# RWKV groups in rounds of three lanes, in one written order on four engines, with an inverse that adds nothing on VectorE

## Chip, cores and metric
The kernel runs on one core of a Trainium2 chip, as one program. The metric is the time of one execution on the device in microseconds (us). The engines are TensorE (PE: matmuls, transposes through the identity; PEld is its weight load), VectorE (DVE), ScalarE (ACT), GpSimd (POOL) and SyncE (SP, which issues the loads of weights).

## What is computed
Two blocks of a network run one after the other over 256 tokens. `first_block` is a feed-forward part, a mixing part and another feed-forward part; the mixing part is attention beside a bidirectional RWKV-7, whose outputs are put side by side and multiplied by `w_out`. The change lies in RWKV-7. Its recurrence over the tokens, for every head and both directions, is

```python
def _rwkv7_step(state, inp):
    r, w, k, v, kk, kka = inp
    sa = einsum('dbhvk,dbhk->dbhv', state, kk)
    state = state * w[..., None, :] - sa[..., :, None] * kka[..., None, :] + v[..., :, None] * k[..., None, :]
    y = einsum('dbhvk,dbhk->dbhv', state, r)
    return state, y
```

with 8 heads of 64, `w` a decay per token and channel (from `wd`, `w2`), `a` a sigmoid (from `ad`, `a2`), `kk` the normalized `k * k_k` and `kka = kk * a`. The two directions are summed, normalized per head (`lnx`), a bonus `v * sum(r * r_k * k)` is added, and all is gated by `sigmoid(gd) @ g2`. `second_block` uses modulation vectors, products of the conditioning `c` with `w_mod`, of which those of its first layer are computed beside the RWKV part.

## The kernel before
**The stage.** `mix1` runs RWKV (`rwkv`) woven with side work: `weave(self.rwkv(...), side, 4)` takes one step of `side` after every four of RWKV's, and what is left of `side` follows. The side work is `mod(0)`: 12 column blocks, each with two loads of 1 MB of `w_mod` (L133, on SP's queue, into `wraw`, which has three buffers), eight matmuls of 32 columns of weights by 512 (L837, four to a load, into the `md` tag of PSUM), a copy `mrow` on ACT (L840), four transposes (L843) and small sums on DVE. Then comes the product with `w_out`: eight loads of 512 KB, each cast by ACT (`whi`, L149) and split by DVE (`wlo`, L150), and 12 matmuls of 512 columns for each (L160 to L162), into `md` and `c2`. Behind it stand a norm and the next feed-forward part.

**The groups.** RWKV is cut into four tiles of 128 channels (`ct`, two heads each) and two directions (`d`), eight groups. A group works on 256 tokens in four chunks of 64. It makes the decay and `a` (matmuls L569 and L570, tanh L573, sigmoid L574, scan L577, exponentials L581 to L591; d=0 also transposes `v` and makes `kk` through two copies `kex`, L558, with a matmul each, L559), products of these (AR, BK, nB, Kh, L594 to L608), and LM, the masked products within a chunk (eight matmuls L623, masks L626). Then it inverts a triangular 64 by 64 matrix for each head and chunk: POOL masks the first level (L654), DVE adds the identity (L656) and transposes (L657), and five levels follow. Each level is two batches of eight quarter matmuls (64 by 64): L663, whose result DVE masks to `FT` (L665), and L670, whose result DVE adds to X (L672) and transposes (L673); the last one adds to Y (L675). Products with the inverse (L680 to L716) follow, and when both directions of a tile are done `finish` runs the chunks' states (L733 to L748), the norm (L751 to L760, with a power on POOL), `fo` (L768 to L770) and the split `xhi`, `xlo` that `w_out` multiplies.

**What sets the order.** The groups are written one after the other with `chain`. The program's scheduler orders the instructions of each engine by its own costs, within the limits of the buffers: the PSUM tags c0, c1, c2, two buffers each, go to the groups in turn by `(2 * ct + d) % DEEP`, with `DEEP = 3`. So work of up to three groups, the side work and `finish` is mixed by the scheduler on each engine's queue, and each engine runs its queue in the order that came out.

Of the kernel before, what the change touches and what calls it, by code (L numbers as in the profile page):

```python
# [20 lines left out]
S = 256  # L21
# [5 lines left out]
LAG = 3  # L27
# [6 lines left out]
class Builder:  # L34
# [473 lines left out]
    def rwkv(self, mp, me, R, yT):  # L508
# [30 lines left out]
        def group(ct, d, sh):  # L539
            tag = "c%d" % ((2 * ct + d) % DEEP)  # L540
            r, k, v = rkv[:, ct], rkv[:, 4 + ct], rkv[:, 8 + ct]
            cc = slice(ct * 128, ct * 128 + 128)
            if d == 0:
                VN = mp.tile([128, 2, 128], F32, name="VN", bufs=2)

                RQ = mp.tile([128, 2, 2, 4, 64], F32, name="RQ", bufs=2)
                vp = self.psum(2, 128, tag=tag)
                for t in range(2):
                    nc.tensor.transpose(vp[:, t], v[:, t * 128:t * 128 + 128], self.ident)
                nc.scalar.copy(VN, vp)  # L550
                for c in range(2):
                    nc.scalar.copy(RQ[halves[1 - c], :, c].rearrange("p d u b -> p d (u b)"),
                                   vp[halves[c]].rearrange("p a b -> p (a b)")[:, None, :].to_broadcast([64, 2, 256]))
                kk = tmpt("kk", 2)
                np_ = self.psum(2, 128, tag=tag)
                for t in range(2):
                    ex = me.tile([128, 2, 64], F32, name="kex", bufs=1)
                    nc.scalar.copy(ex, rn[:, ct, t][:, :, None].to_broadcast([128, 2, 64]))  # L558
                    nc.tensor.matmul(np_[:, t], ex.rearrange("p a b -> p (a b)"), self.ident, start=True, stop=True)  # L559
                nc.vector.scalar_tensor_tensor(kk, k, self.v("rwkv_k_k", ct), np_.rearrange("p a b -> p (a b)"),  # L560
                                               op0=OP.mult, op1=OP.mult)
                sh.update(kk=kk, kds=[], VN=VN, RQ=RQ, Rp=mp.tile([128, 2, 2, 128], F32, name="Rp", bufs=2),
                          y=mp.tile([128, 2, 2, 64], F32, name="y", bufs=2), bv=mp.tile([128, S], F32, name="bv", bufs=2),
                          PZ=mp.tile([128, 2, 3, 2, 64], F32, name="PZ", bufs=2),
                          WC=mp.tile([128, 2, 4], F32, name="WC", bufs=2))
            kk, kds, VN, RQ, PZ, y = (sh[n] for n in ("kk", "kds", "VN", "RQ", "PZ", "y"))
# [8 lines left out]
            sig, a = sa[:, 0], sa[:, 1]  # L575
            cs = tmpt("cs")
            nc.vector.tensor_tensor_scan(cs, rst, sig, 0.0, op0=OP.mult, op1=OP.add)  # L577
            E = me.tile([128, 3, S], F32, name="E")
# [4 lines left out]
            nc.vector.tensor_tensor(less, cs, sig, op=OP.subtract)  # L583
            nc.vector.tensor_tensor(c4(rest), tot.to_broadcast([128, 4, 64]), c4(cs), op=OP.subtract)
            if d == 0:
                nc.scalar.copy(Winc, cs)
            else:
                nc.vector.tensor_tensor(Winc, Wexc, sig, op=OP.add)
            Winv = tmpt("Winv", 2)
            nc.scalar.activation(Winv, Winc, AF.Exp, scale=-KAPPA)  # L590
            nc.scalar.activation(E, E, AF.Exp, scale=KAPPA)  # L591
            kd = tmpt("kd", 2)
            nc.scalar.activation(kd, a, AF.Identity, scale=self.v("rwkv_k_a", ct), bias=ka1[:, ct:ct + 1])
            nc.vector.tensor_tensor(kd, kd, k, op=OP.mult)  # L594
            kds.append(kd)
            nc.gpsimd.tensor_tensor(a, a, kk, op=OP.mult)
            AR = mp.tile([128, 2, 2, 128], F32, name="AR", bufs=3)
            nc.vector.tensor_tensor(AR[:, :, 0], t2v(kk), t2v(Wexc), op=OP.mult)
            nc.vector.tensor_tensor(AR[:, :, 1], t2v(r), t2v(Winc), op=OP.mult)

            BK2 = me.tile([128, 2, 256], F32, name="BK2", bufs=2)
            ch = lambda t: t.rearrange("p (a c b) -> p a c b", c=2, b=64)
            nc.vector.tensor_tensor(BK2.rearrange("p t (j b) -> p t j b", b=64)[:, :, 0:4:3], ch(a), ch(Winv), op=OP.mult)
            nc.vector.tensor_tensor(BK2[:, :, 64:192], t2v(kd), t2v(Winv), op=OP.mult)
            nB = tmpt("nB", 2)
            nc.vector.tensor_tensor(nB, a, Wrem, op=OP.mult)
            Kh = tmpt("Kh", 2)
            nc.gpsimd.tensor_tensor(Kh, kd, Wrem, op=OP.mult)  # L608
            yield

            RHS = mp.tile([128, 4, 128], F32, name="RHS", bufs=DEEP)
            tp = self.psum(2, 2, 64, tag=tag)
            for t in range(2):
                nc.tensor.transpose(tp[:, t].rearrange("p a b -> p (a b)"), AR[:, t, 0], self.ident)
            nc.scalar.copy(RHS.rearrange("p (t h) c -> p t h c", t=2)[:, :, :, 0:64], tp)

# [8 lines left out]
            for hh in range(2):  # L625
                nc.vector.tensor_tensor(LM[:, hh:4:2].rearrange("p t m b -> p t (m b)"), lps[hh],  # L626
                                        lmm[:, d].rearrange("p c m b -> p (c m b)")[:, None, :].to_broadcast([128, 2, 256]), op=OP.mult)
            yield
            tp = self.psum(4, 128, tag=tag)
# [6 lines left out]
            if d == 1:  # L636
                s = tmpt("ksum")
                nc.gpsimd.tensor_tensor(s, kds[0], kds[1], op=OP.add)
                nc.vector.scalar_tensor_tensor(s, s, rk5[:, ct:ct + 1], r, op0=OP.mult, op1=OP.mult)
                bp = self.psum(S, tag=tag)  # L640
                nc.tensor.matmul(bp, blk, s, start=True, stop=True)
                nc.vector.tensor_tensor(sh["bv"], bp, v, op=OP.mult)
            lv = self.psum(4, 64, tag=tag)
            for u in range(4):
                for c in range(2):
                    o = halves[1 - c]
                    nc.tensor.matmul(lv[halves[c], u], LM[o, u, 2 * c], RQ[o, d, c, u], start=True, stop=True)
            nc.scalar.copy(RHS[:, :, 64:128], lv)
# [4 lines left out]
            for c in range(2):  # L653
                nc.gpsimd.tensor_tensor(Y[halves[c]], LM[halves[c], :, 2 * c],  # L654
                                        lvl[halves[c], 0][:, None, :].to_broadcast([64, 4, 64]), op=OP.mult)
            nc.vector.tensor_tensor(Y, Y, over(6), op=OP.add)  # L656
            nc.vector.transpose(X, Y)  # L657
            for li in range(1, 6):
                fp = self.psum(4, 64, tag=tag)
                for u in range(4):  # L660
                    for c in range(2):
                        ps = halves[c]
                        nc.tensor.matmul(fp[ps, u], LM[ps, u, 2 * c], X[ps, u], start=True, stop=True)  # L663
                F = square("FT")
                nc.vector.tensor_tensor(F, fp, over(li), op=OP.mult)  # L665
                yp = self.psum(4, 64, tag=tag)
                l, r_ = (Y, F) if li < 5 else (F, Y)
                for u in range(4):
                    for ps in halves:
                        nc.tensor.matmul(yp[ps, u], l[ps, u], r_[ps, u], start=True, stop=True)  # L670
# [837 lines left out]
def chain(*gens):  # L1508
    for g in gens:
        yield from g  # L1510
# [183 lines left out]
```

## Time and profile before

| | |
|---|---|
| median of three runs | 2453.7 us (2453.59 to 2454.38) |
| profiled execution, its own time | 2451.68 us |
| its span | 2449.9 us |
| PE busy over the span | 2346.6 us (96%) |
| DVE, ACT, POOL busy | 1614.4, 1307.0, 188.2 us |
| mean granted TensorE clock | 0.986 |

The span is from the first to the last instruction. Busy time is a share of all stages together; for a change of one stage the windows of that stage count (the first rows below). Matmuls are pipelined and their ends are modelled, so where a matmul's cost is wanted, the step from one start to the next is safer than its length. Idle time in brackets stands before an instruction and names what ended it.

### The profile page before, as it was taken

What the parts mean: (1) busy time and instruction counts of PE and PEld (TensorE: products, weight loads), DVE (VectorE), ACT (ScalarE), POOL (GpSimd) and SP (SyncE); (2) the same over time, 40 slices, a digit from 0 to 9 for tenths busy, and PEclk for the clock granted to TensorE, in tenths of its full rate; (3) what the DMA queues carried; (4) which work ended last, traced back from release to release, by engine and by line L of the source; (5) the groups of instructions that cost most, each with busy time, mean ns of one, the idle gap of its engine ahead of it and who ended that gap; (6) DMA issues with size and microseconds to landing.
All of it is one profiled execution on the core that took longest, in us unless ns stands there. A gap on an engine that the chain in (4) does not pass through costs nothing. (4 is left out here: it accounts for less than half of the span.)

```text
span 2449.9 us, 38791 instructions
## 1 busy us (share of the span) xinstructions
PE 2346.6 (96%) x15592; PEld 1963.8 (80%) x15592; DVE 1614.4 (66%) x2427; ACT 1307.0 (53%) x2038; POOL 188.2 (8%) x248
## 2 busy tenths in 40 slices
PE   7998989979998999999999999989999999999996
PEld 7996866659998767799899886778888887788875
DVE  5555667656547466443333464669989989889897
ACT  5543644345545355433223243567887777777764
POOL 0001112110001000200100110020100110020000
PEclk9999999999999999999999999999999999999998
DMA  8654342275652350232322235469999999999993
GB/s 261 198 187 138 122 162 88 81 237 170 202 173 88 102 172 21 70 118 82 110 93 82 83 113 175 135 237 373 335 352 341 343 345 335 352 339 335 365 343 134
DMA packets 281100, 489.56 MB, mean 200 GB/s; under 512 B 11424, under 2 KB 116896, under 8 KB 280912
## 3 DMA queue, kind: packets, MB, share of 16 engines
q1 hardware_dynamic: 280832, 486.80, 58.2%
q8 instruction: 124, 2.03, 0.3%
q14 instruction: 64, 0.52, 0.1%
q0 software_dynamic: 80, 0.21, 0.0%
HBM read 485.92 MB, written 1.05 MB: 199 GB/s over the span
## 5 line engine op out<-in xcount | busy, mean ns | idle before, releaser
L150 DVE TENSOR_TENSOR wlo<-wraw,whi 128x1024 fp32r<-128x1024 f32 (+1 forms) x830 | 975.5, 1208 | 227.9 <-ACT whi L149 221.9
L149 ACT CAST whi<-wraw 128x1024 fp32r<-128x1024 f32 (+1 forms) x832 | 824.6, 1030 | 257.9 <-PE ps L162 102.2
L161 PE MATMUL gu<-xlo,whi 128*128 128x256 f32 x1408 | 394.4, 280 | 4.0 <-DVE xlo L193 2.4
L160 PE MATMUL gu<-xhi,whi 128*128 128x256 f32 x1408 | 394.6, 281 | 0.8 <-ACT xhi L200 0.8
L162 PE MATMUL gu<-xhi,wlo 128*128 128x256 f32 x1408 | 393.8, 280 | 0.0
L161 PE MATMUL gu<-wlo,X 128*128 128x512 f32 (+1 forms) x768 | 291.2, 379 | 4.4 <-DVE wlo L150 3.4
L162 PE MATMUL gu<-whi,X 128*128 128x512 f32 (+1 forms) x768 | 286.2, 373 | 0.0
L160 PE MATMUL gu<-whi,X 128*128 128x512 f32 (+1 forms) x768 | 285.1, 374 | 0.0
L161 PEld LDWEIGHTS gu<-xlo,whi 128*128 128x128 f32 x1408 | 264.8, 188 | 5.3 <-DVE xlo L193 2.9
L160 PEld LDWEIGHTS gu<-xhi,whi 128*128 128x128 f32 x1408 | 264.7, 188 | 2.2 <-ACT xhi L200 1.4
L162 PEld LDWEIGHTS gu<-xhi,wlo 128*128 128x128 f32 x1408 | 265.2, 188 | 0.0
L161 PEld LDWEIGHTS gu<-wlo,X 128*128 128x128 f32 x768 | 144.7, 188 | 45.5 <-DVE wlo L150 21.3
L160 PEld LDWEIGHTS gu<-whi,X 128*128 128x128 f32 x768 | 144.7, 188 | 25.5
L162 PEld LDWEIGHTS gu<-whi,X 128*128 128x128 f32 x768 | 144.7, 188 | 23.6
L274 DVE TENSOR_TENSOR hh<-sg,gu 128x256 f32<-128x256 f32 x88 | 36.8, 418 | 164.6 <-ACT sg L272 164.6
L161 PE MATMUL acc<-wlo,xhi 128*128 128x512 f32 (+1 forms) x368 | 141.8, 386 | 3.1 <-DVE wlo L150 3.1
L160 PE MATMUL acc<-whi,xhi 128*128 128x512 f32 (+1 forms) x368 | 140.8, 385 | 2.5 <-ACT whi L149 1.1
L162 PE MATMUL acc<-whi,xlo 128*128 128x512 f32 (+1 forms) x368 | 141.6, 385 | 0.1
L161 PE MATMUL dn<-wlo,hT 128*128 128x512 f32 x352 | 140.6, 399 | 0.0
L162 PE MATMUL dn<-whi,hT 128*128 128x512 f32 x352 | 138.6, 394 | 0.0
L160 PE MATMUL ps<-whi,hhi 128*128 128x512 f32 x352 | 137.2, 390 | 0.0
L162 PE MATMUL ps<-whi,hlo 128*128 128x512 f32 x352 | 137.1, 390 | 0.0
(461 smaller groups left out, 3740.7 us busy)
## 6 DMA issues: line engine op xcount, KB each, us to landing
wraw<-in_exp_w_dram SPq DMA_DIRECT2D x235, 1024.0 KB, 7.0
wraw<-in_w_mod_dram SPq DMA_DIRECT2D x48, 1024.0 KB, 5.2
wraw<-in_w_in_dram SPq DMA_DIRECT2D x29, 1024.0 KB, 5.2
wraw<-in_exp_w_dram SPq DMA_DIRECT2D x58, 512.0 KB, 6.7
wraw<-in_ffn_w_dram SPq DMA_DIRECT2D x28, 1024.0 KB, 5.3
wraw<-in_ffn_w_gate_dram SPq DMA_DIRECT2D x20, 1024.0 KB, 5.7
wraw<-in_ffn_w_up_dram SPq DMA_DIRECT2D x20, 1024.0 KB, 5.5
wraw<-in_ffn_w_down_dram SPq DMA_DIRECT2D x16, 1024.0 KB, 5.1
```

The lines of the kernel that those rows point to most:

```text
L149: nc.scalar.copy(hi, raw[:, k0:k0 + n])
L150: eng.tensor_tensor(lo, raw[:, k0:k0 + n], hi.bitcast(F32), op=OP.subtract)
L160: mm(out, l[0], r[0], start=start, stop=False)
L161: mm(out, l[0], r[1], start=False, stop=False)
L162: mm(out, l[1], r[0], start=False, stop=stop)
L274: nc.vector.tensor_tensor(hh, sg, pg[:, 1], op=OP.mult)
```

## The change
Three things change, all in the RWKV stage.

**Rounds.** `group` and `finish` are cut into more steps by `yield` (a lane, that is a group with its `finish` behind it where d=1, has 22 steps for d=0 and 29 for d=1). `rounds` runs up to three lanes in turn, one step each, then yields once. A new lane starts when a slot is free and at least seven rounds after the last; its PSUM tag goes by slot. All of it, with the woven side steps, stands in `manual_schedule` for PE, DVE, ACT and POOL, so these four keep the order in which the program is written. That gives 204 steps in 90 rounds. Lanes (tile, direction) start in rounds 0, 7, 14, 23, 37, 44, 53 and 60 and end in rounds 22, 36, 36, 52, 59, 73, 75 and 89. `weave` takes a side step after every three rounds.

**Inverse.** The identity is added to LM once (POOL, where it masked the first level before), and the level masks hold the diagonal. So a batch's result holds the sum already: DVE's adds L656, L672, L675 go, and ACT copies from PSUM instead. The first level is now a batch of eight quarter matmuls with the identity and a mask on DVE.

**Order in a group.** The matmuls of the decay come before `kk` and `v`, LM before the transposes of AR, the bonus's matmul after the inverse.

```diff
-LAG = 3
+LAG = 7
...
+                sh.update(VN=VN, RQ=RQ, kds=[], kk=tmpt("kk", 2), Rp=mp.tile([128, 2, 2, 128], F32, name="Rp", bufs=2),
...
+            for c in range(2):
+                m = LM[halves[c], :, 2 * c]
+                nc.gpsimd.tensor_tensor(m, m, lvl[halves[c], 6][:, None, :].to_broadcast([64, 4, 64]), op=OP.add)
+            yield
...
+            quarters = [(u, c) for u in range(4) for c in range(2)]
+            fp = self.psum(4, 64, tag=tag)
+            for u, c in quarters:
+                ps = halves[c]
+                nc.tensor.matmul(fp[ps, u], LM[ps, u, 2 * c], lvl[ps, 6], start=True, stop=True)
             X, Y = square("X"), square("Y")
-
-            for c in range(2):
-                nc.gpsimd.tensor_tensor(Y[halves[c]], LM[halves[c], :, 2 * c],
-                                        lvl[halves[c], 0][:, None, :].to_broadcast([64, 4, 64]), op=OP.mult)
-            nc.vector.tensor_tensor(Y, Y, over(6), op=OP.add)
-            nc.vector.transpose(X, Y)
+            nc.vector.tensor_tensor(X, fp, over(0), op=OP.mult)
...
+            nc.vector.transpose(Y, X)
+            yield
...
             for li in range(1, 6):
                 fp = self.psum(4, 64, tag=tag)
...
                 nc.vector.tensor_tensor(F, fp, over(li), op=OP.mult)
+                yield
                 yp = self.psum(4, 64, tag=tag)
                 l, r_ = (Y, F) if li < 5 else (F, Y)
...
                 if li < 5:
-                    nc.vector.tensor_tensor(X, yp, X, op=OP.add)
+                    X = square("X")
+                    nc.scalar.copy(X, yp)
+                    Y = square("Y")
                     nc.vector.transpose(Y, X)
                 else:
-                    nc.vector.tensor_tensor(Y, yp, Y, op=OP.add)
+                    Y = square("Y")
+                    nc.scalar.copy(Y, yp)
                 yield
...
-        g = [group(ct, d, shs[ct]) for ct in range(4) for d in range(2)]
-        yield from chain(g[0], g[1], finish(0, shs[0]), g[2], g[3], finish(1, shs[1]), g[4], g[5], finish(2, shs[2]), g[6], g[7], finish(3, shs[3]))
+
+        def lane(ct, d):
+            return lambda slot: chain(group(ct, d, shs[ct], slot), finish(ct, shs[ct], slot) if d else iter(()))
+
+        with self.tc.manual_schedule(engines={E.PE, E.DVE, E.Activation, E.Pool}):
+            yield from rounds([lane(ct, d) for ct in range(4) for d in range(2)], DEEP, LAG)
...
-                    yield from weave(self.rwkv(mp, me, R, yT), side, 4)
+                    yield from weave(self.rwkv(mp, me, R, yT), side, 3)
...
+def rounds(lanes, depth, lag):
+
+    todo, active, free, wait = list(lanes), [], list(range(depth)), 0
     while todo or active:
-        if todo and len(active) < depth and wait <= 0:
-            active.append(todo.pop(0))
+        if todo and free and wait <= 0:
+            slot = free.pop(0)
+            active.append((todo.pop(0)(slot), slot))
             wait = lag
         wait -= 1
-        for g in list(active):
+        for a in list(active):
             try:
-                next(g)
+                next(a[0])
             except StopIteration:
-                active.remove(g)
-            yield
+                active.remove(a)
+                free.append(a[1])
+        yield
...
-        lv[:, li] = np.tile(((t // (2 * m) == s // (2 * m)) & (t // m != s // m))[:64, :64], (2, 1))
+        lv[:, li] = np.tile((((t // (2 * m) == s // (2 * m)) & (t // m != s // m)) | (t == s))[:64, :64], (2, 1))
```

How the order moves is seen in three places. On PE late in the stage, before, with the inverse of two groups (L663, L670), the start of a third (L632, L641, L647) and single `md` matmuls of the side work (L837) between:

```order
L663 MATMUL c_5236<-X,LM 64x64 x3
L632 MATMUL c_5426<-k_ident,nB 128x128
L632 MATMUL c_5426<-k_ident,Kh 128x128 x2
L641 MATMUL c_5437<-ksum,k_blk 128x256
L670 MATMUL c_5247<-FT,Y 64x64 x8
L647 MATMUL c_5440<-RQ,LM 64x64 x8
L837 MATMUL md<-wraw,cT 32x512 x4
L663 MATMUL c_5258<-X,LM 64x64 x8
L837 MATMUL md<-wraw,cT 32x512
L663 MATMUL c_5456<-X,LM 64x64 x8
L837 MATMUL md<-wraw,cT 32x512
L670 MATMUL c_5269<-FT,Y 64x64 x8
```

And on PE in a stretch of rounds after the change (L668 and L676 are the two batches of a level, L652 the new first one, L545, L546 and L564 the start of a d=0 lane, L859 the `md` matmuls):

```order
L652 MATMUL c_3503<-k_lvl,LM 64x64 x8
L658 MATMUL c_3515<-RQ,LM 64x64 x8
L668 MATMUL c_3526<-X,LM 64x64 x8
L668 MATMUL c_3538<-X,LM 64x64 x8
L545 MATMUL c_3549<-wd,wag 128x256
L546 MATMUL c_3549<-ad,wag 128x256
L564 MATMUL c_3564<-k_ident,kex 128x128 x2
L859 MATMUL md<-wraw,cT 32x512 x4
L676 MATMUL c_3578<-FT,Y 64x64 x8
L676 MATMUL c_3591<-FT,Y 64x64 x8
L570 MATMUL c_3604<-k_ident,rkv 128x128 x2
L668 MATMUL c_3615<-X,LM 64x64 x8
```

The batches of the lanes now alternate whole, the `md` matmuls of one load stand together, and the two matmuls of `kex` stand ahead of other lanes' batches. On PE behind the states of the last lane (L733, L746 before), before:

```order
L733 MATMUL c_5655<-St,PZ 64x64 x4
L837 MATMUL md<-wraw,cT 32x512 x3
L746 MATMUL c_5663<-St,Rp 64x64 x6
L746 MATMUL c_5671<-St,Rp 64x64 x6
L843 MATMUL md<-k_ident,mrow 128x128 x4
L160 MATMUL md<-whi,xhi 128x512 x2
```

and after (L859 and L865 are the side work, L782 and L783 the last lane's transposes and its `gd` matmul, L160 the first of `w_out`):

```order
L761 MATMUL c_5854<-St,Rp 64x64 x6
L859 MATMUL md<-wraw,cT 32x512 x8
L782 MATMUL c_5888<-k_ident,yn 128x128 x2
L783 MATMUL c_5888<-gd,wag 128x256
L865 MATMUL md<-k_ident,mrow 128x128 x4
L859 MATMUL md<-wraw,cT 32x512 x8
L865 MATMUL md<-k_ident,mrow 128x128 x4
L859 MATMUL md<-wraw,cT 32x512 x8
L865 MATMUL md<-k_ident,mrow 128x128 x4
L160 MATMUL md<-whi,xhi 128x512 x2
```

Two whole column blocks and the end of a third now stand between the last `gd` matmul and `w_out`. On ACT at the same place, before (L149 is the cast of `w_out`, L768 is `fo`):

```order
L840 COPY mrow<-md 128x512
L149 CAST whi<-wraw 128x1024
L755 ACTIVATE yn<-y 128x256
L149 CAST whi<-wraw 128x1024 x2
L768 ACTIVATE fo<-c_5692,k_vec 128x256
L149 CAST whi<-wraw 128x1024
L192 CAST xhi<-fo 128x256
L149 CAST whi<-wraw 128x1024 x4
```

and after:

```order
L770 ACTIVATE yn<-y 128x256
L785 ACTIVATE fo<-c_5888,k_vec 128x256
L192 CAST xhi<-fo 128x256
L862 COPY mrow<-md 128x512 x3
L149 CAST whi<-wraw 128x1024 x8
```

All eight casts moved behind `xhi` and three `mrow` copies. SP's queue holds the same loads, with `grow`, a small constant, three loads of `w_mod` earlier. Outside the stage the order is the same but for buffer numbers.

## Rows read from the trace of the kernel before

**Rows 1.** Windows of the stage: PE, PEld, DVE, ACT, POOL busy; PEclk, DMA, GB/s.
```profile
323.00:350.00 27.00, 21.59 (x194) 11.57 (x190) 19.20 (x46) 18.52 (x43) 6.90 (x12) 0.94 0.69 234
350.00:380.00 30.00, 29.18 (x601) 23.04 (x600) 22.80 (x61) 10.89 (x29) 6.11 (x8) 1.00 0.23 73
380.00:410.00 30.00, 27.95 (x422) 18.28 (x421) 19.67 (x59) 11.53 (x29) 4.45 (x6) 1.00 0.16 43
410.00:440.00 30.00, 28.73 (x491) 20.18 (x490) 21.86 (x63) 11.01 (x28) 6.83 (x9) 1.00 0.31 101
440.00:470.00 30.00, 28.76 (x509) 22.14 (x511) 24.17 (x62) 13.14 (x35) 6.63 (x9) 1.00 0.23 72
470.00:500.00 30.00, 29.28 (x443) 16.52 (x439) 14.21 (x42) 5.70 (x15) 1.90 (x3) 1.00 0.58 186
500.00:520.00 20.00, 17.79 (x195) 10.67 (x193) 9.42 (x25) 8.21 (x15) 2.26 (x2) 1.00 0.74 253
```

**Rows 2.** Groups by line, 323 to 518 us: busy us, mean ns, idle before.
```profile
L837 PE MATMUL md<-wraw,cT 128*32 128x512 f32 x180 | 41.3, 624 | 0.0
L663 PE MATMUL c<-X,LM 64*64 64x64 f32 x640 | 30.6, 223 | 1.0 <-ACT Winv L590 0.4 <-DVE X L657 0.3 <-DVE X L672 0.2
...
L654 POOL TENSOR_TENSOR Y<-LM,k_lvl 64x256 f32<-64x256 f32 x16 | 12.4, 773 | 39.4 <-DVE LM L626 38.8
...
L682 ACT COPY PQ<-c 128x256 f32<-128x256 f32 x8 | 3.0, 370 | 22.6 <-PE c L680 22.6
```

**Rows 3.** Timeline of the last group's inverse: start, us, engine, line, operation.
```profile
493.50 1.07 PE L837 MATMUL md<-wraw,cT 128*32 128x512 f32 x8
...
494.49 0.68 PE L670 MATMUL c<-FT,Y 64*64 64x64 f32 x16
...
495.10 1.06 PE L837 MATMUL md<-wraw,cT 128*32 128x512 f32 x6
495.22 0.42 DVE L672 TENSOR_TENSOR X<-c,X 128x256 f32<-128x256 f32 x1 [1.18 <-PE c L670]
...
497.50 1.04 PE L837 MATMUL md<-wraw,cT 128*32 128x512 f32 x2
...
498.48 0.68 PE L670 MATMUL c<-Y,FT 64*64 64x64 f32 x16
```

**Rows 4.** Timeline of the head, the first groups' preparation.
```profile
323.15 0.70 PE L569 MATMUL c<-wd,wag 64*128 64x256 f32 x2
...
325.69 0.49 PE L559 MATMUL c<-k_ident,kex 128*128 128x128 f32 x2 [1.85 <-ACT kex L558]
...
326.74 0.49 PE L559 MATMUL c<-k_ident,kex 128*128 128x128 f32 x2
...
332.58 0.84 ACT L591 ACTIVATE E<-E 128x768 f32<-128x768 f32 x1
```

**Rows 5.** Timeline of the tail, on ACT and at the end on PE.
```profile
510.65 0.58 ACT L840 COPY mrow<-md 128x512 f32<-128x512 f32 x1 [3.85 <-PE md L837]
511.13 1.05 ACT L149 CAST whi<-wraw 128x1024 fp32r<-128x1024 f32 x1
...
517.49 0.60 PE L766 MATMUL c<-gd,wag 128*128 128x256 f32 x2
518.13 0.56 ACT L768 ACTIVATE fo<-c,k_vec 128x256 f32<-128x256 f32 x1 [2.23 <-PE c L766]
...
537.22 0.40 PE L161 MATMUL c<-wlo,xhi 128*128 128x512 f32 x1
537.45 0.40 PE L162 MATMUL c<-whi,xlo 128*128 128x512 f32 x1
```

**Rows 6.** The page's DMA issues: line, queue, count, KB, us to landing.
```profile
wraw<-in_w_mod_dram SPq DMA_DIRECT2D x48, 1024.0 KB, 5.2
```

**Rows 7.** Windows at the head: columns as in rows 1.
```profile
322.00:326.00 4.00, 2.15 (x16) 0.72 (x8) 2.23 (x8) 2.70 (x7) 0.47 (x4) 1.00 0.61 177
326.00:330.00 4.00, 4.00 (x22) 1.64 (x20) 1.35 (x4) 2.86 (x7) 0.00 (x0) 0.75 0.92 348
```

More of the change, by code (lines that the diff above doesn't have):

```diff
@@ L537, in rwkv, with group @@
         halves = [slice(0, 64), slice(64, 128)]
-        def group(ct, d, sh):
-            tag = "c%d" % ((2 * ct + d) % DEEP)
+        def group(ct, d, sh, slot):
+            tag = "c%d" % slot
             r, k, v = rkv[:, ct], rkv[:, 4 + ct], rkv[:, 8 + ct]
             cc = slice(ct * 128, ct * 128 + 128)
[L543 to L550, printed above, removed]
-                for c in range(2):
[L552 to L566, printed above, removed]
             dr = slice(d * 64, d * 64 + 64)
@@ L638, in group @@
                 nc.gpsimd.tensor_tensor(s, kds[0], kds[1], op=OP.add)
[L639 to L647, printed above, removed]
@@ L648, in group @@
-            nc.scalar.copy(RHS[:, :, 64:128], lv)
+            yield
             square = lambda n, bufs=1: mp.tile([128, 4, 64], F32, name=n, tag=n + tag, bufs=bufs)
             over = lambda i: lvl[:, i][:, None, :].to_broadcast([128, 4, 64])
-            X, Y = square("X"), square("Y")
-            for c in range(2):
-                nc.gpsimd.tensor_tensor(Y[halves[c]], LM[halves[c], :, 2 * c],
-                                        lvl[halves[c], 0][:, None, :].to_broadcast([64, 4, 64]), op=OP.mult)
@@ L658, in group @@
+            for u, c in quarters:
+                o = halves[1 - c]
+                nc.tensor.matmul(lv[halves[c], u], LM[o, u, 2 * c], RQ[o, d, c, u], start=True, stop=True)
+            nc.scalar.copy(RHS[:, :, 64:128], lv)
+            nc.vector.transpose(Y, X)
+            yield
+            if d == 1:
+                nc.vector.scalar_tensor_tensor(s, s, rk5[:, ct:ct + 1], r, op0=OP.mult, op1=OP.mult)
             for li in range(1, 6):
                 fp = self.psum(4, 64, tag=tag)
[L660 to L663, printed above, removed]
+                for u, c in quarters:
+                    ps = halves[c]
+                    nc.tensor.matmul(fp[ps, u], LM[ps, u, 2 * c], X[ps, u], start=True, stop=True)
@@ L664, in group @@
                 F = square("FT")
                 nc.vector.tensor_tensor(F, fp, over(li), op=OP.mult)
+                yield
                 yp = self.psum(4, 64, tag=tag)
                 l, r_ = (Y, F) if li < 5 else (F, Y)
-                for u in range(4):
-                    for ps in halves:
-                        nc.tensor.matmul(yp[ps, u], l[ps, u], r_[ps, u], start=True, stop=True)
+                for u, c in quarters:
+                    ps = halves[c]
+                    nc.tensor.matmul(yp[ps, u], l[ps, u], r_[ps, u], start=True, stop=True)
@@ L684, in group @@
                 nc.scalar.copy(RQ[halves[c], d, c], pp[halves[c], :, 64:128])
+            if d == 1:
+                bp = self.psum(S, tag=tag)
+                nc.tensor.matmul(bp, blk, s, start=True, stop=True)
+                nc.vector.tensor_tensor(sh["bv"], bp, v, op=OP.mult)
             yield
@@ L755, in finish @@
             nc.scalar.activation(z, y, AF.Square)
+            yield
             ss = mp.tile([128, 4], F32, name="mss", bufs=2)
```

73 lines of the change are left out of this document (49 added, 24 removed).

## Prediction
> **What bounds the kernel now.** I read the busy times by window first. From 323.15 us, where the first group's matmul starts [rows 4], to 517.49 us, where the last group's `gd` matmul starts [rows 5], the stage takes 194.4 us, and PE is busy in nearly all of it: 21.59 of the first 27 us, then 27.95 to 29.28 of each 30 us, and 17.79 in the last 20 [rows 1]. Taken up to 517.5 that is about 181 us. DVE is busy 14 to 24 of 30 us, ACT 6 to 13, POOL 2 to 7 [rows 1]. So neither DVE nor ACT bounds this stage; PE does, and the head (323 to 350) is the one stretch where it visibly idles. The groups by line say what fills PE: the side work's `md` matmuls take 41.3 us, the largest entry, before the inverse's L663 with 30.6 [rows 2]. The timeline of one inverse in the last group then says why the side work is that dear: a row of 8 `md` matmuls (four of the program's; the trace has each twice) holds PE 0.99 us (493.50 to 494.49), and a row of 2, a single matmul of the program, holds it 0.98 us (497.50 to 498.48) [rows 3]. By their form each uses 32 columns of the array; four run beside each other in the time of one. The scheduler now cuts most groups of four into one and three, with an inverse step between [rows 3], and so pays nearly twice for them.
>
> So PE's 181 us are about 42 of `md`, 12 times 0.6 of the transposes of `mrow` (an estimate from the matmuls' spacing), 7, and 132 for the lanes. Over 204 lane-steps that is 0.64 us a step, close to the 0.61 us that a batch of quarter matmuls takes from its start to the next matmul (494.49 to 495.10) [rows 3].
>
> **Inverse without sums.** DVE loses in each of eight groups one add of the identity and five adds of 0.42 us [rows 3], and gains one multiplication by a mask, of the same shape, so 5 x 0.42 = 2.1 us a group, 16.8 in all. ACT gains five copies of PSUM of 0.370 [rows 2], 1.85 a group, 14.8 in all. PE gains one batch of quarter matmuls, 0.61 a group [rows 3], 4.9 in all. POOL's two adds of the identity stand in place of its two masks of 0.773 [rows 2]: nothing, though now LM and so the level loop waits for them where Y did. As DVE is far from full, the 16.8 us are worth nothing by themselves; they shorten a chain. A half iteration that ends in the product F costs 0.73 us from the batch's start to the DVE's start (494.49 to 495.22), 0.42 of DVE [rows 3] and a hand-over of about 0.1: 1.2 us. The other half now ends in a copy and not an add: 1.1. That counts only where a lane is alone.
>
> **Side work whole.** The `md` matmuls now go as fours, 0.99 each. `weave` gives one side step in three rounds, 30 in 90 rounds: ten of twelve column blocks lie in the rounds, 20 x 0.99 + 10 x 0.6 = 26 us against 49 now. PE's work in the stage is then 132 + 4.9 + 26 = 163 us against 181. Two column blocks are left for behind it.
>
> **The stage in rounds.** Four engines now keep the written order, lanes start seven rounds apart or later, and the rounds have one lane in 0 to 6, two in 7 to 13, two or three to 74 (one in 36), and one, the last, from 75 on. What the stage takes is then PE's work plus what PE waits, and I walked through it in blocks.
> - Rounds 0 to 13. Lane 00 alone goes through its preparation, serial on ACT and DVE: two `kex` copies with a matmul behind each, which hold PE with idle time of 1.85 us before the first and 1.05 from one to the next, then tanh, sigmoid, scan, two subtractions, the exponential of E (0.84) and the products [rows 4]. From 325.7 (first `kex` matmul) to 333.4 (E done) that is 7.7 us now; the products, LM (eight matmuls) and the mask make it 13. Rounds 7 to 13 repeat that for lane 01 beside the inverse: 13.5. Sum 26.5, of which PE works about 18.
> - Rounds 14 to 75: 170 lane-steps of 0.64, 109, and 17 of side work: 126. To this I add PE's waits. Three times a d=0 lane starts (10, 20, 30): its `kex` matmuls and its E chain stand in the written order before other lanes' batches, and I take 3.2, 6.0 and 4.4 (the dearer ones have one or no second lane in the inverse beside them). Three d=1 starts: 1.9 each, 5.7. Two blocks with finish steps, where DVE and POOL's rsqrt are in turn: 1.7 each, 3.4. Rounds of one or two lanes, where the half iteration of 1.2 us is longer than PE's part: 4.6. Waits 27, sum 153.
> - Last lane alone from round 76 to its `gd` matmul: two half iterations, the steps behind them, and finish. Now 498.48 to 517.5, 19.0 us, with about 4 us of side work between [rows 3]; without the most of that, 15.8.
>
> 26.5 + 153 + 15.8 = 195 us, against 194.4: the stage itself neither gains nor loses, since the 18 us that PE has less to do go into its waits.
>
> **Behind the stage.** Here is a loss that I trust more. Now ACT makes the `mrow` copy of the last column block at 510.65 and the first cast of `w_out` at 511.13, before the last group's `fo` at 518.13; PE's last `w_out` matmul starts at 537.45 [rows 5], 20 us after `gd`. In the new order all eight casts stand on ACT behind `fo`, `xhi` and three `mrow` copies, and on PE all `w_out` matmuls behind two whole column blocks. Counted from the last `gd` matmul: `fo`, its two products and `xhi` 2.5; `mrow` of block 9 0.6, four transposes, so 3.7; block 10: eight `md` matmuls 2.0, `mrow`, transposes, 6.8; block 11: its second load is issued only when block 10's first half has freed a buffer (4.6) and lands 5.2 us later [rows 6], so with its matmuls 10.7, `mrow` to 11.35, transposes 12; first cast to 12.4 and product to 13.7; 96 matmuls at 0.23 (537.22 to 537.45) [rows 5], 22.3. It ends 36 us after `gd`, against 20.4: +15.6. Nothing hides this; what PE does next needs the norm of that product.
>
> **Sum.** 2451.7 (the profiled run, 2.0 under the median) + 0.5 + 15.6 = 2467.8; against the median, 2469.8. Batches that come directly behind each other may cost less than 0.64, by a few us in the middle, and the clock (below) costs about as much: I say 2469.
>
> **Rivals.**
> 1. *The forecast*: rounds leave PE some 27 us of waits in the middle, and the tail adds 15.6. With the waits at 15 or 40 us, 2457 to 2482. Chance 0.55.
> 2. *Rounds pack* (faster or level). Three lanes of 0.61 and a quarter of a side step make 2.1 us, longer than the half iteration's 1.2, so each result is there before its lane's turn; if preparation also hides in the rounds of the two others, PE stays as full as now in the middle (29 of 30 [rows 1]): 126 / 0.96 = 131, stage 173, and 2453.7 - 21.1 + 15.6 = 2448. With each of the 110 batches there a tenth under its 0.61, it is 2441. It decides where the waits fall under 12 us in 62 rounds. For it: the lanes are seven rounds apart, so their dear steps seldom meet. Against: one written order on four engines has no other work to slip in when a d=0 lane waits for its exponential. Chance 0.28: 0.17 faster, 0.11 level.
> 3. *Rounds stall*. An engine in the written order takes nothing from behind a waiting instruction; a preparation step that is late on ACT holds the other lanes' copies, these hold PE, and each round costs the sum of its hand-overs, 2.8 us: 62 x 2.8 = 174, 2490. Now, too, PE idles 1.85 us before `kex` with matmuls of another group directly behind [rows 4]. [...] Chance 0.09.
> 4. *Clock*. [...] Chance 0.08 beyond what the forecast holds.
>
> **How the numbers follow.** 0.2%, 4.9 us, is what a measurement of this kernel can tell from no change: 2449 to 2459. Slower is rivals 3 and 4 and the forecast but 0.03 of it: 0.69. Level is 0.11 and 0.03, 0.14; faster 0.17. The range of 2446 to 2486 leaves out the better half of rival 2 and most of rival 3.
>
> **What would show it.** Right: `md` matmuls at some 1.0 us per four, 18 us less PE busy before the last `gd` matmul, which still starts near 518; the first cast of `w_out` some 11 us behind it, the last `w_out` matmul near 554. Wrong: the last `gd` matmul before 502, or PE 95% busy from round 14 on (rival 2); idle time of PE in every round (rival 3); a granted clock under 1 between 323 and 350 and again from 500 on for more than 8 us (rival 4). If the `md` records still stand in parts, the order isn't what the change says.

## The result: slower by 35 us, and the profile after

The changed kernel takes 2489.3 us (2487.5 to 2490.9), the kernel before 2453.8: a ratio of 1.0143, with a 95% interval of 1.0129 to 1.0157. The forecast, 2469 with a range of 2446 to 2486, had the sign and less than half of the size. The profiled execution has a span of 2486.9 us against 2449.9, 37.0 more.

The stage by windows in the kernel after, with the columns of [rows 1]:

```profile
323.00:350.00 27.00, 13.96 (x116) 8.44 (x116) 11.18 (x28) 11.79 (x27) 5.28 (x10) 0.67 0.24 78
350.00:380.00 30.00, 23.55 (x366) 17.25 (x364) 14.36 (x39) 11.37 (x29) 3.86 (x5) 0.78 0.22 71
380.00:410.00 30.00, 26.57 (x610) 20.51 (x608) 19.14 (x51) 12.68 (x36) 5.23 (x8) 1.00 0.34 108
410.00:440.00 30.00, 24.04 (x410) 16.20 (x405) 14.17 (x38) 13.26 (x38) 4.20 (x6) 0.89 0.33 107
440.00:470.00 30.00, 22.87 (x346) 17.24 (x346) 16.26 (x45) 11.19 (x27) 4.95 (x7) 0.75 0.22 72
470.00:500.00 30.00, 26.16 (x494) 19.98 (x490) 17.98 (x47) 16.07 (x42) 5.61 (x8) 0.91 0.23 72
500.00:530.00 30.00, 23.11 (x546) 17.32 (x542) 13.89 (x43) 9.22 (x27) 2.12 (x4) 1.00 0.49 158
530.00:550.00 20.00, 13.61 (x92) 4.77 (x92) 5.53 (x19) 2.53 (x6) 1.21 (x2) 0.66 0.60 197
```

Two columns differ. PE idles: from 323 to 530 its busy time is 160.3 of 207 us, so 46.7 us idle. And the granted clock, 0.94 in the first window of [rows 1] and 1.00 in all others, is 0.67 to 0.91 in five of seven windows here. In windows of 1 us the granted clock is 0.50 or 1.00, except where it changes. So a mean of 0.67 over 27 us is 18 us at 0.50, and the five windows make 58 us of that. So the 160 us of busy time also hold work at half the rate: a group of four `md` matmuls took 1.93 to 1.94 us where the clock was 0.50 throughout, and 1.06 to 1.07 where it was 1.00.

What PE waited for, from the first lane's start to the last `gd` matmul (engine, line, releaser: us in total, times, longest):

```profile
PE md L865 <- ACT mrow L862: 15.9, 7, 5.1
PE c L564 <- ACT kex L563: 12.1, 8, 5.0
PE c L620 <- DVE AR L609: 3.4, 1, 3.4
PE c L676 <- DVE FT L670: 3.1, 7, 0.7
...
PE c L668 <- ACT X L679: 1.8, 3, 1.1
```

The inverse (L668, L676) is hardly in it. Two copies on ACT are: `mrow`, for which the side work's transposes wait, and `kex`. In the kernel before, up to its last `gd` matmul, the longest entries hold none for `mrow` and 1.8 us for `kex`. The timeline of the head shows how both come late:

```profile
320.91 0.70 PE L545 MATMUL c<-wd,wag 64*128 64x256 f32 x2
...
326.20 0.63 ACT L550 ACTIVATE sa<-sa 128x512 f32<-128x512 f32 x1
326.73 0.28 ACT L563 COPY kex<-rn 128x128 f32<-128x128 f32 x1
327.07 0.79 PE L564 MATMUL c<-k_ident,kex 128*128 128x128 f32 x2 [5.03 <-ACT kex L563]
...
329.40 1.94 PE L859 MATMUL md<-wraw,cT 128*32 128x512 f32 x8
...
341.12 0.70 PE L545 MATMUL c<-wd,wag 64*128 64x256 f32 x2
...
342.18 0.68 PE L668 MATMUL c<-X,LM 64*64 64x64 f32 x16
...
346.60 0.84 ACT L595 ACTIVATE E<-E 128x768 f32<-128x768 f32 x1
347.35 0.57 ACT L862 COPY mrow<-md 128x512 f32<-128x512 f32 x1
...
347.98 1.12 PE L865 MATMUL md<-k_ident,mrow 128*128 128x128 f32 x4 [5.11 <-ACT mrow L862]
349.02 1.12 PE L676 MATMUL c<-FT,Y 64*64 64x64 f32 x16
...
360.71 0.70 PE L545 MATMUL c<-wd,wag 64*128 64x256 f32 x2
```

`kex` needs nothing of this lane, but stands behind the lane's tanh and sigmoid on ACT, and PE stands still until 327.07. (That tanh itself waited for `hb`, a small constant that DVE makes, until 325.33.) The matmuls that `mrow` copies are done by 339, but it stands in ACT's order behind the second lane's exponential of E (L595), which needs four steps of DVE; PE has the transposes next in its order and waits until 347.98, with the first lane's batch L676 behind them ready since 344.9 (its `FT` ends at 344.88). From lane 1 to 2 to 3 (the three L545) it takes 20.2 and 19.6 us. And the four `md` matmuls at 329.40, after the idle 5 us, take 1.94 us at a clock of 0.50, where such a row takes 1.07 in [rows 3].

The tail, which begins with the last `gd` matmul:

```profile
536.91 1.06 PE L783 MATMUL c<-gd,wag 128*128 128x256 f32 x2
538.01 0.56 ACT L785 ACTIVATE fo<-c,k_vec 128x256 f32<-128x256 f32 x1 [3.98 <-PE c L783]
...
540.53 1.12 PE L865 MATMUL md<-k_ident,mrow 128*128 128x128 f32 x4 [2.56 <-ACT mrow L862]
541.58 3.08 PE L859 MATMUL md<-wraw,cT 128*32 128x512 f32 x16
...
544.73 12.29 SPq L133 DMA_DIRECT2D wraw<-in_w_out_dram  x6
...
548.74 1.06 PE L859 MATMUL md<-wraw,cT 128*32 128x512 f32 x8 [1.66 <-DMA wraw<-in_w_mod_dram]
...
551.55 0.19 DVE L867 TENSOR_REDUCE modT<-md 128x8 f32<-128x32 f32 x1 [5.04 <-PE md L865]
551.60 1.04 ACT L149 CAST whi<-wraw 128x1024 fp32r<-128x1024 f32 x1 [1.09 <-DMA wraw<-in_w_out_dram]
552.70 1.22 PE L160 MATMUL md<-whi,xhi 128*128 128x512 f32 x2 [1.18 <-ACT whi L149]
...
577.33 0.39 PE L162 MATMUL c<-whi,xlo 128*128 128x512 f32 x1
```

With the side work that is left behind in between, `w_out` starts on PE 15.8 us after `gd`. What ends last there is the load of `w_out`, issued from 544.73 on behind those of `w_mod`, for which the first cast waits until 551.60; the last read of the PSUM tag `md` by the side work (L867) is done at about the same time. The last matmul of `w_out` starts 40.4 us after `gd`, against 20.0 in [rows 5]. So the stage loses 19.4 us up to `gd` (536.91 against 517.49) and the tail 20.5; of these 39.9, 2.9 are won back by the end of the span, and it isn't shown where.

### The profile page after: what moved, and what is told of

It reads as the page before. It is cut to its first block, busy times and chain, and to the rows that moved or that the text cites. A ratio compares the mean times of both kernels' runs of the same rounds, so it can differ in the third digit from the quotient of the medians.

```text
span 2486.9 us, 39072 instructions
## 1 busy us (share of the span) xinstructions
PE 2342.2 (94%) x15720; PEld 1966.4 (79%) x15720; DVE 1599.6 (64%) x2387; ACT 1320.7 (53%) x2078; POOL 185.6 (7%) x248
## 5 line engine op out<-in xcount | busy, mean ns | idle before, releaser
L149 ACT CAST whi<-wraw 128x1024 fp32r<-128x1024 f32 (+1 forms) x832 | 824.5, 1030 | 262.0 <-PE ps L162 102.4
L160 PE MATMUL gu<-xhi,whi 128*128 128x256 f32 x1408 | 394.2, 281 | 0.8 <-ACT xhi L200 0.8
L160 PE MATMUL gu<-whi,X 128*128 128x512 f32 (+1 forms) x768 | 285.2, 374 | 0.0
L160 PEld LDWEIGHTS gu<-xhi,whi 128*128 128x128 f32 x1408 | 264.0, 188 | 2.2 <-ACT xhi L200 1.4
L160 PEld LDWEIGHTS gu<-whi,X 128*128 128x128 f32 x768 | 144.8, 188 | 25.6
L160 PE MATMUL acc<-whi,xhi 128*128 128x512 f32 (+1 forms) x368 | 140.8, 385 | 2.4 <-ACT whi L149 1.1
L160 PE MATMUL ps<-whi,hhi 128*128 128x512 f32 x352 | 137.2, 390 | 0.0
```

Source lines behind the costliest of these rows:

```text
L149: nc.scalar.copy(hi, raw[:, k0:k0 + n])
L160: mm(out, l[0], r[0], start=start, stop=False)
```

## The experiments

All were timed against the kernel before on the same chip. The last column is the ratio less one times 2453.7 us. The intervals are 0.10 to 0.17% wide to each side, 2.5 to 4 us.

| kernel | ratio | interval | us against before |
|---|---|---|---|
| changed kernel | 1.0143 | 1.0129 to 1.0157 | +35 |
| before, new inverse alone | 1.0042 | 1.0028 to 1.0057 | +10 |
| changed, old inverse | 1.0150 | 1.0133 to 1.0167 | +37 |
| changed, scheduler orders all engines | 0.9967 | 0.9955 to 0.9980 | -8 |
| the same, old inverse | 0.9954 | 0.9943 to 0.9965 | -11 |
| changed, only PE in the written order | 1.0030 | 1.0017 to 1.0042 | +7 |
| changed, only ACT left to the scheduler | 1.0041 | 1.0024 to 1.0058 | +10 |
| changed, `mrow`'s transposes a side step later | 1.0127 | 1.0110 to 1.0144 | +31 |
| changed, `kex` copies ahead | 1.0117 | 1.0100 to 1.0134 | +29 |
| changed, a side step in two rounds | 1.0088 | 1.0071 to 1.0105 | +22 |
| the same and `mrow` | 1.0059 | 1.0042 to 1.0076 | +14 |
| the same, `mrow` and `kex` | 1.0006 | 0.9996 to 1.0016 | +1.5 |
| the three edits, only PE in the written order | 0.9983 | 0.9973 to 0.9993 | -4 |
| the three edits, old inverse | 0.9988 | 0.9978 to 0.9998 | -3 |
| the three edits, lanes four rounds apart | 1.0030 | 1.0017 to 1.0042 | +7 |
| changed, idle matmuls in thin rounds | 1.0274 | 1.0257 to 1.0291 | +67 |
| changed, idle matmuls in three waits | 1.0142 | 1.0126 to 1.0159 | +35 |

**Inverse or order.** The first five kernels take the change apart. The inverse alone, put into the chained groups of the kernel before, with the same masks as in the change:

```diff
+            for c in range(2):
+                m = LM[halves[c], :, 2 * c]
+                nc.gpsimd.tensor_tensor(m, m, lvl[halves[c], 6][:, None, :].to_broadcast([64, 4, 64]), op=OP.add)
...
+                    nc.tensor.matmul(fp[ps, u], LM[ps, u, 2 * c], lvl[ps, 6], start=True, stop=True)
+            nc.vector.tensor_tensor(X, fp, over(0), op=OP.mult)
...
-                    nc.vector.tensor_tensor(X, yp, X, op=OP.add)
+                    X = square("X")
+                    nc.scalar.copy(X, yp)
...
```

> The kernel before with the new inverse alone (identity added to LM, eight more quarter matmuls, ACT copies in place of DVE adds); groups chained and ordered by the scheduler as before, one side step after four. Theory A (the written order on four engines costs the time, the inverse is neutral): 2452 to 2459 us, PE being the bound and having 5 us more to do. Rival B (the inverse's ACT copies and the longer first level cost): 2465 or more.

It took 10 us more, between what the two theories gave. Its last `gd` matmul starts at 526.03 us against 517.49, with hardly a wait of PE for the new inverse's copies on ACT (0.7 us in three times). The granted clock is lower in it than before (0.77 from 410 to 440 us, where it was 1.00), and by the prediction's estimate PE has 4.9 us more to do; the rest of the 10 us isn't settled.

The changed kernel with the scheduler's order:

```diff
-        with self.tc.manual_schedule(engines={E.PE, E.DVE, E.Activation, E.Pool}):
-            yield from rounds([lane(ct, d) for ct in range(4) for d in range(2)], DEEP, LAG)
+        yield from rounds([lane(ct, d) for ct in range(4) for d in range(2)], DEEP, LAG)
```

> The changed kernel without the fixed order: rounds of three lanes, new inverse and a side step in three rounds are written as they are, but the scheduler orders all engines. Theory A: most of the 35 us goes, 2448 to 2462. Rival B: 2470 or more. Rival C (it is the rounds, with one or two lanes at the ends, that thin the work out, whatever orders it): 2470 or more as well, with PE idle in the first 40 us of the stage as in the changed kernel.

This is the main finding: 8 us faster than before, 43 less than with the written order, from the same instructions, and under the range that theory A gave. Its windows:

```profile
323.00:350.00 27.00, 21.42 (x231) 11.82 (x230) 21.00 (x48) 19.36 (x47) 9.13 (x15) 1.00 0.50 166
350.00:380.00 30.00, 29.87 (x670) 24.41 (x666) 19.48 (x53) 13.52 (x38) 3.88 (x6) 1.00 0.19 65
380.00:410.00 30.00, 28.31 (x506) 19.65 (x502) 19.63 (x54) 16.73 (x44) 5.16 (x7) 1.00 0.42 142
410.00:440.00 30.00, 28.14 (x510) 19.63 (x510) 21.64 (x59) 14.54 (x39) 6.56 (x9) 1.00 0.23 73
440.00:470.00 30.00, 30.00 (x625) 22.17 (x621) 20.80 (x59) 13.53 (x37) 7.56 (x10) 1.00 0.39 128
470.00:500.00 30.00, 27.02 (x432) 15.39 (x431) 11.43 (x39) 8.55 (x24) 1.20 (x2) 1.00 0.65 218
```

PE idles 12.2 of 177 us, and the granted clock is 1.00 in every window. The last `gd` matmul starts at 499.42, and that of `w_out` at 526.01. The `md` matmuls are split again here: 94 of them take 38.6 us up to the last `gd`, where the changed kernel's 80, in twenty groups of four, cost 27.6, in part at a granted clock of 0.50 (1.94 us a group there, 1.07 at 1.00). So whole groups, the greater part of the 18 us that PE was to have less to do, are worth less than a PE that does not wait.

The old inverse, with its masks on POOL and its adds on DVE, in the fixed order, and with the scheduler:

> The changed kernel with the old inverse (POOL masks, DVE adds), rounds and fixed order as they are. Theory A: as slow as the changed kernel, 2482 to 2495. Rival B: it gets back what the copies cost, 2475 or less.

> Rounds written as in the changed kernel, the scheduler ordering all engines, and the old inverse. If the new inverse costs under the scheduler what it did in the chained kernel (10 us): 2432 to 2438. If it is neutral, as in the fixed order: 2441 to 2447. If it is what gains: 2450 or more.

2490.2 and 2440.5 us. In the fixed order the inverse makes no difference; with the scheduler the old one is as fast or a little faster. Rounds, with the scheduler's order and the old inverse, have the lowest time of all kernels here, 0.46% under the kernel before. Rival B falls for the changed kernel: the 35 us are the order's.

**Which engine's order.**

```diff
-        with self.tc.manual_schedule(engines={E.PE, E.DVE, E.Activation, E.Pool}):
+        with self.tc.manual_schedule(engines={E.PE}):
```

> The changed kernel with the written order kept on PE alone; DVE, ACT and POOL are ordered by the scheduler. If it is PE's order that holds ready batches behind waiting instructions: 2480 to 2492, as the changed kernel. If it is ACT's and DVE's order that makes kex, mrow and the copies late: 2450 to 2465.

```diff
-        with self.tc.manual_schedule(engines={E.PE, E.DVE, E.Activation, E.Pool}):
+        with self.tc.manual_schedule(engines={E.PE, E.DVE, E.Pool}):
```

> The changed kernel with the written order kept on PE, DVE and POOL; ACT alone is ordered by the scheduler. With PE's order alone fixed it took 2459 us, with all four 2489. If ACT's written order makes kex, mrow and the copies late: 2457 to 2465. If DVE's does as much: 2470 to 2480. If DVE's alone does it: 2485 or more.

2458.8 and 2465.3. With ACT alone left to the scheduler, 25 of the 35 us are gone; with DVE and POOL left to it too, another 3 (within the intervals), and with PE as well, another 15. ACT's order was not fixed by itself, so its 25 us are what it costs beside the orders of the other three. What PE waited for with ACT free, where the row of `mrow` is gone from the list and `kex` is halved:

```profile
PE c L564 <- ACT kex L563: 6.2, 5, 2.0
PE c L676 <- DVE FT L670: 6.1, 7, 1.8
PE c L620 <- DVE AR L609: 3.4, 1, 3.4
```

**Which waits.** Three edits leave the four engines in the written order and move only what was late. The transposes and sums of a column block go, as `flush`, to the start of the next block's first side step (one side step behind the copy `mrow`); the `kex` copies go ahead of the tanh, into two buffers; `weave` takes a side step every second round:

```diff
         for cb in cbs:
+            if last is not None:
+                flush(*last)
             p = self.psum(512, tag=tag)
...
             nc.scalar.copy(rows, p)
+            last = (cb, rows)
             yield
```
```diff
+            if d == 0:
+                exs = [me.tile([128, 2, 64], F32, name="kex", bufs=2) for t in range(2)]
+                for t in range(2):
+                    nc.scalar.copy(exs[t], rn[:, ct, t][:, :, None].to_broadcast([128, 2, 64]))
             pw = self.psum(2, S, tag=tag)
...
-                for t in range(2):
-                    ex = me.tile([128, 2, 64], F32, name="kex", bufs=1)
-                    nc.scalar.copy(ex, rn[:, ct, t][:, :, None].to_broadcast([128, 2, 64]))
+                for t, ex in enumerate(exs):
```
```diff
-                    yield from weave(self.rwkv(mp, me, R, yT), side, 3)
+                    yield from weave(self.rwkv(mp, me, R, yT), side, 2)
```

> The changed kernel, the side work's transposes of mrow one side step later (three rounds behind the copy that they wait for), nothing else. PE stood idle for mrow 20 us in all, some 11 of them before the last gd matmul. Theory A1 (waits in the written order hold PE directly): these 11 us go, and some of the half-rate time with them, 2470 to 2480 us. Rival: the wait only passes to what stands next in the order: 2485 to 2490.

> The changed kernel, the two kex copies of a d=0 lane made on ACT ahead of the tanh of the same step, into two buffers, so that PE's kex matmuls find them done; nothing else. PE stood idle for kex 12.1 us in eight waits. If these waits are on the path: 2477 to 2481. If what stands behind them is late anyway: 2486 to 2490.

> The changed kernel with a side step after every second round, so that all twelve column blocks lie in the rounds and none is left behind the last lane. If the two blocks behind it cost what the prediction said (about 10 of the 36 us between the last gd matmul and the last w_out matmul) and the rounds take them in their idle time: 2477 to 2480. If each block costs the rounds as much as it does behind them: 2487 to 2490. If the transposes of mrow hold PE in the rounds for 2 us a block more: 2484.

> The two edits together: a side step after every second round, and the transposes of mrow a side step later. If side work left behind and waits for mrow are two causes that add: 15 us from the first and about 12 from the second, 2458 to 2464. If they are one: 2472 to 2475.

> Three edits together: a side step after every second round, the transposes of mrow a side step later, the kex copies ahead. If the three add: the 21 us of the first two and 8 to 12 of the third, 2456 to 2460. If the order's other waits (of the inverse's batches for DVE and ACT) take what kex gives back: 2465 to 2468.

Alone `mrow`, `kex` and the side step give 4, 6 and 13.5 us (2483.3, 2480.5, 2473.9), `mrow` and the side step together 21 (2467.6), and all three 34: 2452.7, the time of the kernel before. The sum of the single gains is 24, so the waits had hidden each other: with `mrow` alone mended, PE's waits for `FT` and X rise from 4.9 to 9.2 us. The expectations had these sizes wrong: `mrow` alone and `mrow` with the side step came out between their two ranges, the side step alone and the three together below all of theirs. In the kernel with all three edits, PE's longest entries are now the inverse's own:

```profile
PE c L678 <- DVE FT L672: 4.5, 8, 1.4
PE c L670 <- ACT X L681: 4.2, 6, 1.6
PE c L691 <- ACT Y L686: 3.1, 4, 1.6
PE c L715 <- DVE Rp L709: 2.2, 4, 0.8
PE c L622 <- DVE AR L611: 2.2, 2, 2.0
PE c L566 <- ACT kex L547: 2.0, 1, 2.0
```

The side step in two rounds did more than to bring two blocks under cover. With the side work done before the last lane ends, `w_out` starts ahead of `gd`, here in the kernel with this edit alone:

```profile
529.14 0.73 PE L160 MATMUL md<-whi,xhi 128*128 128x512 f32 x2
...
543.54 0.60 PE L783 MATMUL c<-gd,wag 128*128 128x256 f32 x2
...
556.51 0.40 PE L162 MATMUL c<-whi,xlo 128*128 128x512 f32 x1
```

The last lane ends 6.6 us later than in the changed kernel, `w_out` 13.0 us behind it and not 40.4. I had weighed only the blocks' own 10 us. Two things are free earlier: the PSUM tag `md`, into which `w_out` multiplies, and the queue of loads (the first `w_out` matmul starts at 529.14, so its load had landed by then, where that load was issued only at 544.73 in the changed kernel). No run separates them.

**What is left.** On top of the three edits:

> Side steps after every second round, mrow's transposes a side step later, kex copies ahead, and the written order kept on PE alone. If the gains of the free engines (30 us) and of the three edits (36 us) are the same waits seen twice: 2448 to 2455. If they add in part: 2435 to 2445.

> The three edits in the order fixed on four engines, with the old inverse (DVE adds, POOL masks). If the inverse is neutral there too: 2450 to 2456. If DVE's 17 us less count now that PE waits less: 2458 or more. If its eight more matmuls a group on PE count: 2446 to 2449.

> The three edits in the order fixed on four engines, lanes starting four rounds apart or later where it was seven. The stage has fewer rounds with one lane at its head. If these thin rounds cost time of their own: 3 to 8 us less, 2445 to 2450. If the preparation of three lanes then meets on ACT and PE waits for it: 2453 or more.

2448.0, 2449.2 and 2458.8. Freeing ACT, DVE and POOL gives another 5 to 6 us, where it gave 28 without the edits: mostly the same waits. The old inverse is 4 us faster, at the edge of the intervals; DVE's 17 us less count for nothing here either. Lanes closer together (`LAG = 4`) are slower by 6 and not faster: PE then waits 5.7 us for `St` and 3.5 for RHS on ACT. So fewer thin rounds at the head gave nothing back in sum; what they cost by themselves isn't shown.

**The clock.** Two kernels put matmuls that nothing reads into PE's order; the expectation of the second takes 0.49 us for each, and nine of them took 4.15 us there at a granted clock of 1.00, 0.46 each. Three at the end of every round with a free PSUM tag:

```diff
+        if free:
+            fill(free[-1])
         yield
```

> The changed kernel with three matmuls of 256 columns that nothing reads at the end of every round in which one of the three PSUM tags is free (36 of the 90 rounds), so that PE is kept at work where lanes are few: about 30 us more of PE time at the full rate. Theory A2 (the clock: PE at half its rate for 65 of the stage's 216 us is a cause of its own): the granted clock of the stage rises to 0.95 or more and the time falls to 2470 to 2482. Rival (the clock is only a sign of the waits, in which its rate does not matter): 2489 or more.

These were 126 matmuls. Three of them took 1.46 to 1.56 us at a granted clock of 1.00 and 2.73 at 0.50, so with 0.52 for each I estimate 66 us and not 30. The time rose by 32: by this estimate about half found a place in waits, half did not. The time lies where the rival was to put it, but the added matmuls themselves can have brought it there, so the clock question stays open by it. So, second, 24 of them in the three longest waits of the head, 9, 6 and 9:

```diff
+            if (ct, d) == (0, 0):
+                fill(9)
```

> The changed kernel with 24 matmuls of 256 columns that nothing reads, each 0.49 us at the full rate, put into the three longest waits of PE in the head: 9 ahead of the first kex matmul (wait of 5.03 us), 6 ahead of the first LM matmuls (3.41), 9 ahead of the first mrow transposes (5.11). PE is at half its rate for some 24 of the head's 40 us there. If that rate costs time of its own, the granted clock from 321 us on stays near 1, the third lane's first matmul comes 3 to 6 us earlier than 39.8 us after the first lane's, and the time is 2483 to 2486. If not: 39 to 41 us and 2488 to 2491.

The head by windows, the changed kernel's two rows first, then this one's:

```profile
321.00:341.00 20.00, 11.11 (x80) 6.10 (x80) 8.51 (x21) 8.15 (x20) 3.84 (x8) 0.66 0.21 61
341.00:361.00 20.00, 13.78 (x207) 10.48 (x202) 9.98 (x25) 6.86 (x16) 3.62 (x5) 0.74 0.27 94
```
```profile
321.00:341.00 20.00, 16.56 (x135) 11.74 (x134) 9.31 (x24) 10.05 (x24) 4.30 (x9) 1.00 0.32 106
341.00:361.00 20.00, 15.45 (x227) 10.65 (x227) 9.31 (x24) 6.25 (x16) 3.17 (x5) 0.93 0.18 55
```

With 11.2 us more work, the granted clock is 1.00 and 0.93 where it was 0.66 and 0.74, and the third lane starts 34.8 us after the first (353.83 less 319.04) and not 39.8. So the lower clock has a price of its own, 5 us of these 40, which idle matmuls win back in this profiled execution. The time as a whole moved from 1.0143 to 1.0142, so a gain of this size in the end isn't shown.

## Why the prediction was wrong

**What bounds the kernel now**: right for the middle. PE bounds the stage, and DVE's relief was worth nothing: the old inverse in the fixed order makes no difference (1.0150 against 1.0143). But "ACT 6 to 13" leaves out the head, where [rows 1] has ACT busy 18.52 of 27 us; there the copies on ACT were what came late.

**Side work whole**: the count was right, its price not. Twenty groups took 27.6 us, not 19.8: twelve took 1.06 to 1.07 each, and the other eight, where the granted clock was 0.50 for all or part of their time, 14.8 together.

**The stage in rounds**: here the sum failed, 195 us predicted against 216.0 measured (320.91 to 536.91).

| block | predicted | measured |
|---|---|---|
| first L545 to the first `kex` matmul | not in the sum | 6.2 |
| from there to the second lane's L545 (rounds 0 to 6) | 13 | 14.1 |
| from there to the third lane's L545 (rounds 7 to 13) | 13.5 | 19.6 |
| from there to the last `gd` | 153 + 15.8 | 176.2 |
| from `gd` to the end of `w_out`'s last matmul | 36 | 40.8 |

The step that failed is PE's waits for copies on ACT, and the lower granted clock that came with them (0.66 and 0.74 in the head, against 1.00 and 0.93 with idle matmuls in its waits).

- The transposes of `mrow` stood in the sum with 0.6 us of work a block and no wait, although they stand directly behind a copy on an ACT queue that was now fixed. PE waited 15.9 us for them before the last `gd`, 5.11 of it in rounds 7 to 13. The term "Waits 27" has lines for `kex` at the later starts, and none for `mrow`.
- I priced the first `kex` wait by [rows 4], where ACT had made the copy ahead of the tanh; in the written order it stands behind, which the order's rows on ACT would have told, and PE waited 5.03 us and not 1.85. The 13 us of rounds 0 to 6 were counted from the first `kex` matmul, so the stretch ahead of it was missing: 2.5 us in the kernel before, 6.2 here, of which 2.2 are only an earlier start (320.91 against 323.15).
- The clock was set against closer batches and left at nothing; no run shows that term. What the runs showed in its place is some 58 us between 323 and 530 at a granted clock of 0.50. What that costs over the whole stage no run shows; in the head it was 5 us in one profiled execution.

The three edits give back 34 of 35 us, but not all of it where it was lost: with them the last `gd` starts at 521.35, 15.6 us earlier than in the changed kernel and still 3.9 later than before, and the last `w_out` matmul 14.6 us behind it, 5.4 less than before. So they show that late copies and left-over side steps made most of the loss, and not that they made all of the 19.4 us in the stage.

**Behind the stage**: the mechanism was right (two blocks on PE and eight casts on ACT behind the last lane), and its 15.6 us measured 20.5; `mrow` waits there too (2.56 us at 540.53), and the first `w_out` matmuls ran at a granted clock of 0.50 (552 to 556), one every 0.42 to 0.43 us and not every 0.23. That the same blocks also hold `w_out` off, by their PSUM tag or their loads, I had not seen.

**Rivals.** Rival 2 was wrong for the written order and right for the steps: ordered by the scheduler, the rounds do pack, 0.33% under the kernel before. Rival 3 (one late item on ACT holds the others and PE) was nearest, with a chance of 0.09: it named the engine and the mechanism, but I priced it as every round's hand-over, while it is the waits for `mrow` (seven) and `kex` (eight) before the last `gd`. That its 2490 lies beside the measured 2489.3 is luck: it has 174 us for rounds 14 to 75 and 15.8 for the last lane, and the two together took 176.2. When ACT alone was left to the scheduler, 25 us went. The trace of the changed kernel shows ACT keeping its order: the matmuls that `mrow` copies were done by 339, ACT idled 1.30 us up to 346.11, and the copy ran at 347.35, behind the exponential that stands ahead of it (346.60). Rival 4, the clock, had a chance of 0.08. Its sign was met in the head (0.67 from 323 to 350) and behind `gd` (0.66 from 530 to 550), but also in the middle (0.89, 0.75 and 0.91 from 410 to 500), where the prediction did not look for it. In the changed kernel it goes with rival 3: after the first wait for `kex` the four `md` matmuls behind it were slower too (1.94 us against 1.07).

**How the numbers follow.** Rivals 3 and 4 were set as alternatives to the forecast. As I read the runs, they are in the main one cause and its consequence and should have moved the forecast itself, and the range's upper end to 2500. But the kernel with the new inverse alone also had a lower clock (0.77 from 410 to 440 us) where PE waited only 1.1 us for `mrow` and 1.9 for `kex`, and that stays open.

## What to carry to other kernels

A written order on several engines is only as good as its latest item on each: walk every engine's queue by itself and ask, for each copy that another engine waits for, what stands ahead of it there and what that needs. Put a step's producer one step or more ahead of its consumer when both queues are fixed; here `kex` ahead of the tanh, the transposes a side step behind `mrow` and an earlier side step were worth 34 us. The new inverse gained nothing in any order, and in the chained groups of the kernel before it cost 10 us. If you can, first try the new steps in the scheduler's order: that separates what the steps are worth from what the order costs.

## What the runs showed that I had not expected

PE's clock fell in the middle of a busy-looking stage. Two windows of 1 us in the changed kernel, with the columns of [rows 1]:

```profile
326.00:327.00 1.00, 0.00 (x0) 0.00 (x0) 0.00 (x0) 0.97 (x3) 0.00 (x0) 0.50 0.00 0
...
335.00:336.00 1.00, 1.00 (x11) 1.00 (x12) 0.00 (x0) 0.00 (x0) 0.00 (x0) 0.50 0.84 326
```

The clock fell while PE idled up to 327.07, and stayed at 0.50 to 339, also where PE was busy throughout. In between four `md` matmuls took 1.94 us and not 1.07. Four windows of 30 us with 22.87 to 26.16 us of busy time had a granted clock of 0.75 to 0.91, though the one from 500 to 530, with 23.11, had 1.00. So in this stage the busy share itself misleads: part of it is the same work at a granted clock of 0.50. Idle matmuls in the waits held the clock at 1.00 and 0.93 in the head, where it was 0.66 and 0.74.
